# A VectorE duration table, the rank of LayerNorm sums and the place of one product chunk in a Conformer and MLP kernel

## The chip, the core and the metric

One core of a Trainium2 chip runs the whole kernel. It has a matrix engine (TensorE, PE in the rows), a vector engine (VectorE, DVE), an activation engine (ScalarE, ACT), a general engine (GpSimd, POOL) and DMA queues that SyncE (SP) fills. Each engine works through its own list of instructions in order; between engines, semaphores make an instruction wait for what it reads or overwrites. The metric is the device time of one execution in microseconds (us), the median of several runs. Beside the runs stands one profiled execution, and every row below is from that one.

## What is computed

One layer: adaLN modulation, a Conformer convolution module and a squared-ReLU MLP on 1024 tokens of 1024 channels, all in float32. The tokens form segments of 64, and the depthwise convolution stays inside a segment.

```
mod = silu(c) @ w_mod + b_mod          # shift, scale, gate, twice
h = rms_norm(x, norm1_g) * (1 + s1) + sh1
u = h @ w_pw1 + b_pw1                  # pointwise, 1024 -> 2048
a, gate = split(u, 2); u = a * sigmoid(gate)
u = dwconv(u, w_dw) + b_dw             # 31 taps, segments of 64 tokens
u = silu(layer_norm(u, ln_g, ln_b))
x = x + g1 * (u @ w_pw2 + b_pw2)
h = rms_norm(x, norm2_g) * (1 + s2) + sh2
x = x + g2 * (square(relu(h @ w1)) @ w2)   # 1024 -> 4096 -> 1024
out = rms_norm(x, final_g)
```

## The kernel before, in words

**Tiles.** Channels lie on the 128 partitions, tokens along the free side. The tokens form two blocks, A (`b` = 0) and B (`b` = 1), of 512 each; the 1024 channels are eight chunks `c` of 128. A tile `small` is one chunk of one block (128x512), a `bank` one accumulator of PE, a `big` tile a 128x1024 piece of weights or a pair of `small` ones. Each float32 product is three matmuls of parts: hi by hi, hi by lo, lo by hi (L429, L430, L431). "One product" below means these three. The hi part is a cast (weights L391, activations L371 or L568, on ACT), the lo part a subtraction (L378 or L572, on DVE or POOL).

**Stages.** (1) Modulation (L587 on DVE, L595 with L600 on POOL and ACT) and the first RMSNorm. (2) The first pointwise product, a chunk at a time: `first(b, c)` makes 2 x 8 products, which fill two banks, and `gate(b, c)` makes their GLU, a sigmoid on ACT (L631) and a multiplication on DVE (L640). `PW1_ORDER` lists the chunks that run before LayerNorm A; those of `PW1_LATE`, (1, 2) and (1, 3), have a late rank. (3) The depthwise convolution of block A, beside stage 2: of the 31 taps of a chunk, some are diagonal matmuls on PE (`matrix_tap`, L687), some products of ACT (L717) with sums on POOL (L722), the rest multiply-adds of DVE that go in turn to two banks (L732). DVE closes a chunk with two sums (L742, L751). (4) LayerNorm A: `cmean[0]` is a `Mean`. POOL adds the finished chunks 0 to 5 up (L378 on `small` tiles), and PE sums that total, chunk 6 and chunk 7 over the channels, in three feeds of a matrix of ones (L451, two rows of the trace each). DVE subtracts the mean eight times (L766), ACT squares (L493), PE feeds the eight squares (L451 again), ACT takes a root (L505), DVE a reciprocal (L507). 22 small matmuls (L544) stand on PE between. DVE then multiplies (L780), ACT makes the SiLU (L785) and the hi part (L371), DVE the lo part (L378). (5) The second pointwise product of block A: eight output chunks `j` of eight products, each added to x by DVE (L800). (6) The second RMSNorm of A, `norm2`: two feeds on PE (L451), root, reciprocal, L553 and L568 for hi, L572 for lo. (7) The MLP's first product of A (32 chunks, to HBM), with convolution, LayerNorm and second pointwise product of B beside it. (8) The MLP's second product for both blocks, then the final norm.

**The order.** The kernel is not issued in the order in which it is written. Each operation goes into a `plan` with a cost in nanoseconds for its engine (`c_dve`, `c_stt`, `c_act`, `c_pool`) and a rank, `prio`: the number last given to `plan.at`, or one of its own, as the matrix taps have (1030). `plan.run` plays the kernel through with those costs. Whenever an engine is free it takes the operation of the lowest rank among those whose inputs are there in that play. The result is a fixed list for each engine; when the kernel runs, nothing is chosen anew. So a changed cost or rank shows only as another order. Ranks: 1030 matrix taps, 1100 to 1109 the chunks of `PW1_ORDER`, 1200 convolution A, 1300 LayerNorm A, 1400 to 1407 the second pointwise product, 1500 `norm2`, 1600 the late chunks, 2000 on the MLP and block B.

Of the kernel before, what the change touches and what calls it, by code (L numbers as in the profile page):

```python
# [15 lines left out]
KC = D // P  # L16
# [24 lines left out]
PW1_ORDER = (  # L41
    (0, 4), (0, 5), (1, 0), (1, 4), (1, 5),
    (0, 6), (0, 7), (1, 6), (1, 7), (1, 1),
)
PW1_LATE = ((1, 2), (1, 3))
CONV_B = (0, 3, 6, 9, 12, 15, 18, 21)
# [8 lines left out]
CM = (2, 1)  # L55
# [7 lines left out]
S2_ENG, G1_ENG = ("pool", "pool", "dve", "pool", "pool", "pool", "pool", "pool"), ("pool", "pool", "pool", "dve", "dve", "pool", "dve", "pool")  # L63
SH2_ENG, G2_ENG = ("dve", "dve", "dve", "dve", "dve", "dve", "dve", "dve"), "dve"
G1_GATE, S2_GATE = None, None

# [179 lines left out]
def trunk(  # L246
# [50 lines left out]
    def c_dve(n):  # L297
        return 67 + 1.045 * n

    def c_stt(n):  # L300
        return 127 + 1.045 * n

# [137 lines left out]
    class Mean:  # L440

        def __init__(self, b, direct=1, eng="pool", turned=False):
            self.b, self.direct, self.eng, self.turned = b, direct, eng, turned
            self.n, self.sum, self.own, self.acc = 0, None, False, None

        def feed(self, x, first, last):
# [12 lines left out]
            if self.turned:  # L461
                plan.op("pe", 450 * QT, emit_turned, [x, ones], banks(self.acc))
            else:
                plan.op("pe", 1.67 * TB[self.b], emit, [x, ones], banks(self.acc))

# [151 lines left out]
    us, cv, begun = {}, {}, {}  # L617
    cmean = [Mean(0, CM[0]), Mean(1, CM[1])]

# [40 lines left out]
    def conv_start(b, c):  # L660

        u = us[b, c]
        after = [cv[b, c - 2]] if c > 1 else []

        def first_tap(dst, at, k, s):
# [93 lines left out]
    def layer_norm(b, direct):  # L759
        ms = Mean(b, direct, turned=TURNED[1 + 2 * b])  # L760
        for c in range(KC):
# [325 lines left out]

    def first(b, c):
        out = []
        for h in range(2):  # L1090
            acc = acc_of(b, unit=SEG)
            if c < KEPT:
                w_of[c, h] = [wf[k][2 * c + h] for k in range(KC)]
            elif (c, h) not in w_of:
                w_of[c, h] = weights(wpw1[2 * c + h], PW1_LO, (), h1[0][KC - 1 :])
            products(acc, w_of[c, h], h1[b])
            out.append(acc)
        gate(b, c, *out)

    for n, bc in enumerate(PW1_ORDER):  # L1100
        plan.at(1100 + n)
        first(*bc)
    plan.at(1200)
# [142 lines left out]
```

## Time and profile before

| what | value |
|---|---|
| median of 3 runs | 1022.71 us (1021.47 to 1023.96) |
| the profiled execution, its own time | 1022.33 us |
| its span in the trace | 1020.5 us |
| PE busy, share of the span | 980.4 us, 96% |
| DVE busy | 757.2 us, 74% |
| ACT busy | 520.1 us, 51% |
| POOL busy | 513.8 us, 50% |

The profile gives for each engine how long it was busy in a stretch, and the clock granted to PE as a share of full speed. A timeline row has the start, the time, the engine, the source line and operation, what is written and read, and how many instructions were joined. A bracket at its end is idle time just before it, with the instruction that ended it. PE's matmuls overlap: a row of 0.39 us next to one that starts 0.227 us later costs PE 0.227 us. DVE's neighbours overlap a little too, so the cost of a step is the distance between two starts.

### The profile page before, as it was taken

The page shows a single profiled execution, that of the slowest core. Times are in us where ns is not written, and L with a number is a line of the kernel's source. Part 1 is how long each engine was busy: PE and PEld are TensorE (multiplying, and loading weights), DVE is VectorE, ACT ScalarE, POOL GpSimd, SP SyncE. Part 2 cuts the span into 40 slices and gives each one's busy share as a digit, 9 for nine tenths or more (in the row PEclk, how much of TensorE's full clock was granted, in tenths as well). Part 3 has the DMA queues.
Part 4 walks back from the last instruction along what each step waited for, and adds up shares of the span by engine and source line. Part 5 has one row for each costly group of instructions (what it writes and reads, how often), then busy time and mean ns, then how long its engine had stood idle before and what let it go on. Part 6 is the DMA issues. An engine that isn't in the chain of part 4 may idle for free.

```text
span 1020.5 us, 11766 instructions
## 1 busy us (share of the span) xinstructions
PE 980.4 (96%) x4210; PEld 791.7 (78%) x4210; DVE 757.2 (74%) x1008; ACT 520.1 (51%) x748; POOL 513.8 (50%) x328
## 2 busy tenths in 40 slices
PE   5999999959999999999999999999999999999994
PEld 4878787638888888788888888888888888888882
DVE  5999999999699999863464473664747466494887
ACT  6488755185567765582473334342333434252443
POOL 0049999157744544322365536536363653634444
PEclk7999999979999999999999999999999999999998
DMA  9930025444426543644152413123141212303004
GB/s 358 404 114 1 1 83 208 163 164 165 145 83 215 182 158 116 224 157 155 67 192 87 141 41 104 62 83 124 62 144 42 99 66 83 125 1 124 1 1 165
DMA packets 52523, 125.28 MB, mean 123 GB/s; under 512 B 4464, under 2 KB 21104, under 8 KB 52464
## 3 DMA queue, kind: packets, MB, share of 16 engines
q1 hardware_dynamic: 52464, 124.53, 34.7%
q8 instruction: 33, 0.54, 0.2%
q14 instruction: 26, 0.21, 0.1%
HBM read 111.93 MB, written 12.58 MB: 122 GB/s over the span
## 4 chain that ended last, share of the span: by engine, by line
PE 75%; DVE 19%; POOL 2%; issue 2%; ACT 1%; DMA 1%; SPq 0%; POOLq 0%; DVEq 0%; ACTq 0%
PE bank L430 14%; PE bank L431 14%; PE bank L429 14%; DVE bank L732 12%; PE bank L913 10%; PE bank L914 10%; PE bank L912 10%; PE bank L451 2%; DVE big L378 1%; POOL small L378 1%; DVE bank L507 1%; DVE small L751 1%; POOL small L722 1%; DVE big L587 1%; DVE small L640 1%
## 5 line engine op out<-in xcount | busy, mean ns | idle before, releaser
L378 POOL TENSOR_TENSOR big<-big 128x1024 fp32r<-128x1024 f32 (+1 forms) x124 | 299.0, 2421 | 339.0 <-DVE big L378 155.6
L429 PE MATMUL bank<-big 128*128 128x512 f32 x896 | 355.0, 396 | 4.1 <-ACT big L371 3.9
L430 PE MATMUL bank<-big 128*128 128x512 f32 x896 | 350.0, 391 | 4.3 <-DVE big L378 3.2
L431 PE MATMUL bank<-big 128*128 128x512 f32 x896 | 349.7, 390 | 0.0
L800 DVE SCALAR_TENSOR_TENSOR small<-bank,mod,small 128x512 f32<-128x512 f32 x240 | 176.6, 748 | 197.1 <-PE bank L914 158.3
L378 DVE TENSOR_TENSOR big<-big 128x1024 fp32r<-128x1024 f32 (+2 forms) x160 | 198.6, 1262 | 27.4 <-POOL big L378 9.7
L872 ACT CAST big<-big 128x1024 fp32r<-128x1024 f32 x112 | 113.4, 1050 | 193.8 <-POOL big L378 60.0
L430 PEld LDWEIGHTS bank<-big 128*128 128x128 f32 x896 | 168.8, 188 | 42.8 <-DVE big L378 3.7
L732 DVE SCALAR_TENSOR_TENSOR bank<-small,vec,bank 128x464 f32<-128x464 f32 (+11 forms) x318 | 200.5, 697 | 1.7
L429 PEld LDWEIGHTS bank<-big 128*128 128x128 f32 x896 | 168.9, 188 | 41.8 <-ACT big L371 4.1
L431 PEld LDWEIGHTS bank<-big 128*128 128x128 f32 x896 | 168.8, 188 | 35.2
L912 PE MATMUL bank<-big 128*128 128x512 f32 x448 | 174.7, 390 | 0.0
L913 PE MATMUL bank<-big 128*128 128x512 f32 x448 | 174.3, 389 | 0.0
L914 PE MATMUL bank<-big 128*128 128x512 f32 x448 | 174.3, 389 | 0.0
L722 POOL TENSOR_TENSOR small<-small 128x400 f32<-128x400 f32 (+4 forms) x109 | 113.3, 1067 | 50.4 <-DVE big L378 27.8
L391 ACT CAST big<-big 128x1024 fp32r<-128x1024 f32 x92 | 95.6, 1043 | 23.4 <-POOL big L378 11.0
L912 PEld LDWEIGHTS bank<-big 128*128 128x128 f32 x448 | 84.1, 188 | 17.7 <-issue 0.2
L913 PEld LDWEIGHTS bank<-big 128*128 128x128 f32 x448 | 84.1, 188 | 17.6 <-issue 0.2
L914 PEld LDWEIGHTS bank<-big 128*128 128x128 f32 x448 | 84.1, 188 | 17.4
L378 POOL TENSOR_TENSOR small<-small 128x512 f32<-128x512 f32 x39 | 52.1, 1340 | 83.3 <-DVE big L378 44.3
L493 ACT ACTIVATE small<-small 128x512 f32<-128x512 f32 x64 | 39.0, 628 | 64.2 <-DVE small L800 60.0
L717 ACT ACTIVATE small<-small,vec 128x400 f32<-128x400 f32 (+4 forms) x109 | 62.9, 629 | 0.0
(68 smaller groups left out, 597.6 us busy)
## 6 DMA issues: line engine op xcount, KB each, us to landing
big<-in_w SPq DMA_DIRECT2D x96, 512.0 KB, 3.9
big<-in_wmod SPq DMA_DIRECT2D x48, 512.0 KB, 5.4
big<-in_wpw SPq DMA_DIRECT2D x28, 512.0 KB, 5.3
hidden<-small SPq DMA_DIRECT2D x32, 256.0 KB, 2.4
big<-hidden SPq DMA_DIRECT2D x16, 512.0 KB, 3.9
small<-in_xA SPq DMA_DIRECT2D x16, 256.0 KB, 5.2
big<-in_wfirst SPq DMA_DIRECT2D x8, 512.0 KB, 10.2
small<-in_xB SPq DMA_DIRECT2D x16, 256.0 KB, 6.1
```

The costliest lines, as they stand in the source:

```text
L378: lambda: eng_of[o.eng].tensor_tensor(out=out(), in0=a(), in1=b(), op=op), r, w, part=part, port=port,
L391: plan.op("act", c_act(D), lambda: act.copy(t(wh), t(raw)), [raw], [wh], also=[wl])
L429: pe.matmul(o, wh, hi(a)[:, s], start=first, stop=False)
L430: pe.matmul(o, wh, lo(a)[:, s], start=False, stop=False)
L431: pe.matmul(o, wl, hi(a)[:, s], start=False, stop=last)
L722: return pool.tensor_tensor(out=dst, in0=dst, in1=seg(t(m))[:, :, tt], op=ALU.add)
L732: dve.scalar_tensor_tensor(out=dst, in0=src, scalar=w, in1=dst, op0=ALU.mult, op1=ALU.add)
L800: lambda s=s, p=p: dve.scalar_tensor_tensor(out=t(x)[:, s], in0=cut(s, p), scalar=scale.t, in1=t(x)[:, s], op0=ALU.mult, op1=ALU.add,),
L872: plan.op("act", c_act(D), lambda: act.copy(t(h), t(x)), [x], [h], also=[l])
L912: pe.matmul(t(p), t(wh)[:, cs], t(hh)[:, ns], start=first and k == 0, stop=False, skip_group_check=not first)
L913: pe.matmul(t(p), t(wh)[:, cs], t(hl)[:, ns], start=False, stop=False, skip_group_check=not first)
L914: pe.matmul(t(p), t(wl)[:, cs], t(hh)[:, ns], start=False, stop=k == 1, skip_group_check=not first)
```

## The change

Three things change; a fourth, `HOLD_B`, is off and does nothing.

- Chunk (1, 2) leaves `PW1_LATE` and becomes the eleventh of `PW1_ORDER`, with rank 1110; the loads of its weights now wait until chunk (1, 1) has been gated.
- A `Mean` can carry a rank. The three feeds of `cmean[0]` and the eight feeds of LayerNorm A's squares get 1030, above the first product's chunks.
- The plan's cost of a DVE two-operand step rises by 8 ns, that of a DVE multiply-add by 23 ns.

```diff
 PW1_ORDER = (
     (0, 4), (0, 5), (1, 0), (1, 4), (1, 5),
-    (0, 6), (0, 7), (1, 6), (1, 7), (1, 1),
+    (0, 6), (0, 7), (1, 6), (1, 7), (1, 1), (1, 2),
 )
-PW1_LATE = ((1, 2), (1, 3))
+PW1_LATE = ((1, 3),)
+PW1_BACK = 1
...
     def c_dve(n):
-        return 67 + 1.045 * n
+        return 75 + 1.045 * n
...
     def c_stt(n):
-        return 127 + 1.045 * n
+        return 150 + 1.045 * n
...
-        def __init__(self, b, direct=1, eng="pool", turned=False):
+        def __init__(self, b, direct=1, eng="pool", turned=False, prio=None):
+            self.prio = prio
...
-                plan.op("pe", 1.67 * TB[self.b], emit, [x, ones], banks(self.acc))
+                o = plan.op("pe", 1.67 * TB[self.b], emit, [x, ones], banks(self.acc))
+                if self.prio:
+                    o.prio = self.prio
...
-    cmean = [Mean(0, CM[0]), Mean(1, CM[1])]
+    cmean = [Mean(0, CM[0], prio=1030), Mean(1, CM[1])]
...
     def layer_norm(b, direct):
-        ms = Mean(b, direct, turned=TURNED[1 + 2 * b])
+        ms = Mean(b, direct, turned=TURNED[1 + 2 * b], prio=1030 if b == 0 else None)
...
-    def first(b, c):
+    def first(b, c, after=()):
...
-                w_of[c, h] = weights(wpw1[2 * c + h], PW1_LO, (), h1[0][KC - 1 :])
+                w_of[c, h] = weights(wpw1[2 * c + h], PW1_LO, after, h1[0][KC - 1 :])
...
-        first(*bc)
+        first(*bc, [us[PW1_ORDER[n - PW1_BACK]]] if n >= 10 else ())
```

No instruction is added or dropped: only the lists' order changes. In the lists below each row is a source line, an operation, what it writes and reads, its shape, and how many stand in a row.

**DVE, from the end of convolution A to the reciprocal of LayerNorm A, before.** L751 (not shown) has just closed chunk 7; L587 is a modulation step, L732 a tap of block B, L640 the gate of chunk (1, 1), L766 the eight subtractions of the mean, L507 the reciprocal:

```order
L587 ISA big,mod<-big,csil,vec 128x1024
L587 ISA mod 128x1
L1121 TENSOR_SCALAR g1b<-mod,vec 128x1
L732 SCALAR_TENSOR_TENSOR bank<-small,vec,bank 128x8x54
L732 SCALAR_TENSOR_TENSOR bank<-small,vec,bank 128x8x55 x2
L732 SCALAR_TENSOR_TENSOR bank<-small,vec,bank 128x8x56
L640 SCALAR_TENSOR_TENSOR small<-bank,vec,small 128x8x64
L732 SCALAR_TENSOR_TENSOR bank<-small,vec,bank 128x8x56
L732 SCALAR_TENSOR_TENSOR bank<-small,vec,bank 128x8x57
L766 TENSOR_TENSOR small<-small,bank 128x512 x8
```

Ahead of these rows and behind L751 stand three more modulation steps and five column steps (L610, L1121). The same stretch after; the lines are 5 to 7 higher there (L758 closes chunk 7, L773 subtracts, L512 is the reciprocal, L645 the gate, L787 the multiplication):

```order
L758 TENSOR_TENSOR small<-bank,small 128x512
L592 ISA big,mod<-big,csil,vec 128x1024
L592 ISA mod 128x1
L615 TENSOR_SCALAR sc_88<-mod,vec 128x1
L1128 TENSOR_SCALAR g1b<-mod,vec 128x1
L773 TENSOR_TENSOR small<-small,bank 128x512 x8
L739 SCALAR_TENSOR_TENSOR bank<-small,vec,bank 128x8x55 x2
L739 SCALAR_TENSOR_TENSOR bank<-small,vec,bank 128x8x56 x2
L592 ISA big,mod<-big,csil,vec 128x1024
```

Two more modulation steps and a column step follow, then these:

```order
L512 RECIPROCAL bank<-bank 128x512
L645 SCALAR_TENSOR_TENSOR small<-bank,vec,small 128x8x64
L787 TENSOR_TENSOR small<-small,bank 128x512 x8
L1128 TENSOR_SCALAR g1b<-mod,vec 128x1
L615 TENSOR_SCALAR sc_88<-mod,vec 128x1
L739 SCALAR_TENSOR_TENSOR bank<-small,vec,bank 128x8x57
L380 TENSOR_TENSOR big<-small,big 128x512 x3
```

Between the end of the convolution and the subtractions only one modulation step and two column steps are left; one of the six taps and two column steps now stand ahead of L758, the gate of (1, 1) behind the reciprocal. Between subtractions and reciprocal there were two modulation steps, two column steps and five taps; now there are three, one and four.

**PE, at LayerNorm A, before:** all products of `PW1_ORDER`, then the eleven feeds (L451), then the small matmuls:

```order
L431 MATMUL bank<-big 128x512
L451 MATMUL bank<-small,ones 128x512 x11
L544 MATMUL bank<-ones 128x128 x11
L429 MATMUL bank<-big 128x512
```

After, two of the feeds (L454 there) stand far ahead, among the matrix taps (L694) and products of chunks 6 and 7. This is the first of them, for the total of chunks 0 to 5:

```order
L694 MATMUL bank<-small,diag 128x8x51 x2
L694 MATMUL bank<-small,diag 128x8x52
L454 MATMUL bank<-small,ones 128x512
L694 MATMUL bank<-small,diag 128x8x52
L431 MATMUL bank<-big 128x512
```

The feed of chunk 7 stands four products before the end of the first product; three of them follow it, then come the feeds of the squares, the last product and the small matmuls:

```order
L433 MATMUL bank<-big 128x512
L454 MATMUL bank<-small,ones 128x512 x8
L431 MATMUL bank<-big 128x512
L432 MATMUL bank<-big 128x512
L433 MATMUL bank<-big 128x512
L549 MATMUL bank<-ones 128x128 x11
```

The 16 products of chunk (1, 2) stand, after, inside the second pointwise product of A (behind 21 of its 64). Behind the last feed of `norm2` there were 30 products of late chunks; now there are 14.

**DVE, ahead of the reciprocal of `norm2`, after:**

```order
L592 ISA big,mod<-big,csil,vec 128x1024
L592 ISA mod 128x1
L807 SCALAR_TENSOR_TENSOR small<-bank,mod,small 128x512
L380 TENSOR_TENSOR big<-big 128x1024 x2
L512 RECIPROCAL bank<-bank 128x512
L558 SCALAR_TENSOR_TENSOR small<-small,sc_88,bank 128x512 x4
L577 SCALAR_TENSOR_TENSOR big<-small,mod,big 128x512 x4
```

L807 is the last addition to x. Before, a modulation step stood in the place of the two weight splits (L380), and the lo part (L572 there, L577 here) began behind three multiplications instead of four.

## Rows read from the trace of the kernel before

**Rows 1.** Windows: from:to, length, busy us (instructions) by engine, PEclk, DMA share, GB/s.

```profile
65.00:200.00 135.00, 134.47 (x549) 102.31 (x548) 131.91 (x205) 84.83 (x156) 111.97 (x99) 1.00 0.24 85
200.00:234.00 34.00, 20.54 (x60) 11.96 (x59) 33.08 (x56) 25.31 (x40) 16.42 (x11) 0.75 0.42 144
234.00:998.00 764.00, 763.30 (x3348) 627.90 (x3347) 523.71 (x642) 365.64 (x486) 373.09 (x207) 1.00 0.31 108
```

**Rows 2.** Timeline of PE through LayerNorm A.

```profile
199.39 0.39 PE L431 MATMUL bank<-big 128*128 128x512 f32 x1
199.62 2.74 PE L451 MATMUL bank<-small,ones 128*128 128x512 f32 x6
208.66 9.15 PE L451 MATMUL bank<-small,ones 128*128 128x512 f32 x16 [6.30 <-ACT small L493]
...
224.19 0.80 PE L429 MATMUL bank<-big 128*128 128x512 f32 x1 [3.92 <-ACT big L371]
228.23 0.79 PE L430 MATMUL bank<-big 128*128 128x512 f32 x1 [3.24 <-DVE big L378]
```

**Rows 3.** Timeline of DVE, from the end of convolution A.

```profile
197.27 0.20 DVE L610 TENSOR_SCALAR sc<-mod,vec 128x1 f32<-128x1 f32 x1
...
205.27 0.75 DVE L640 SCALAR_TENSOR_TENSOR small<-bank,vec,small 128x512 f32<-128x512 f32 x1
205.93 1.28 DVE L732 SCALAR_TENSOR_TENSOR bank<-small,vec,bank 128x448 f32<-128x448 f32 x2
207.12 4.87 DVE L766 TENSOR_TENSOR small<-small,bank 128x512 f32<-128x512 f32 x8
211.90 1.28 DVE L587 CUSTOM_DVE_ANT_0 big<-big,csil,vec 128x1024 f32<-128x1024 f32 x1
213.10 0.09 DVE L587 DVE_READ_ACCUMULATOR2_ANT mod<- 128x1 f32 x1
...
218.55 3.37 DVE L507 RECIPROCAL bank<-bank 128x512 f32<-128x512 f32 x1 [0.85 <-ACT bank L505]
221.95 4.87 DVE L780 TENSOR_TENSOR small<-small,bank 128x512 f32<-128x512 f32 x8
226.74 0.21 DVE L610 TENSOR_SCALAR sc<-mod,vec 128x1 f32<-128x1 f32 x1
...
227.48 2.50 DVE L378 TENSOR_TENSOR big<-small,big 128x512 fp32r<-128x512 f32 x4
```

**Rows 4.** Chain of waits: start, us, link; taps that follow on one bank.

```profile
132.36 0.70 DVE bank L732
...
133.09 0.71 DVE bank L732
```

**Rows 5.** Timeline of ACT: the last sigmoid before convolution A ends.

```profile
188.94 0.69 ACT L631 ACTIVATE small<-bank,vec 128x512 f32<-128x512 f32 x1 [7.64 <-PE bank L431]
```

**Rows 6.** Timeline of DVE: that sigmoid's gate.

```profile
194.58 0.75 DVE L640 SCALAR_TENSOR_TENSOR small<-bank,vec,small 128x512 f32<-128x512 f32 x1
```

**Rows 7.** Timeline of POOL: the total of chunks 0 to 5, and `norm2`.

```profile
165.35 1.26 POOL L378 TENSOR_TENSOR small<-small 128x512 f32<-128x512 f32 x1
...
272.64 4.72 POOL L378 TENSOR_TENSOR big<-big 128x1024 fp32r<-128x1024 f32 x2
```

**Rows 8.** Timeline of DVE at `norm2`.

```profile
274.95 3.49 DVE L587 CUSTOM_DVE_ANT_0 big<-big,csil,vec 128x1024 f32<-128x1024 f32 x1
...
278.38 3.35 DVE L507 RECIPROCAL bank<-bank 128x512 f32<-128x512 f32 x1
...
283.75 0.75 DVE L572 SCALAR_TENSOR_TENSOR big<-small,mod,big 128x512 fp32r<-128x512 f32 x1
...
293.00 4.63 DVE L378 TENSOR_TENSOR big<-big 128x1024 fp32r<-128x1024 f32 x4
```

**Rows 9.** Timeline of PE at `norm2`: its two feeds.

```profile
274.02 1.02 PE L451 MATMUL bank<-small,ones 128*128 128x512 f32 x2
...
276.25 1.02 PE L451 MATMUL bank<-small,ones 128*128 128x512 f32 x2
```

More of the change, by code (lines that the diff above doesn't have):

```diff
@@ L64 @@
 SH2_ENG, G2_ENG = ("dve", "dve", "dve", "dve", "dve", "dve", "dve", "dve"), "dve"
+HOLD_B = False
 G1_GATE, S2_GATE = None, None
@@ L663, in conv_start @@
         after = [cv[b, c - 2]] if c > 1 else []
+        if b == 1 and c == 0 and HOLD_B:
+            after = [cmean[0].acc[0][1]]
         def first_tap(dst, at, k, s):
```

## Prediction

> **What bounds the kernel now.** I read the windows first. From 65 to 200 us PE is busy 134.47 of 135 us, from 234 to 998 us 763.30 of 764, both at a granted clock of 1.00; from 200 to 234 us it is busy 20.54 of 34 us, at 0.75 [rows 1]. The change neither adds nor drops an instruction, so PE can win only what it loses now, and that lies in one place, LayerNorm A. The timeline of PE says who it waits for there: 6.30 us for ACT's squares, 3.92 us for the first hi part, 3.24 us for the first lo part [rows 2]. These look like three causes. The timeline of DVE shows that they are one queue. Convolution A is done when DVE issues the next thing at 197.27, yet the subtractions of the mean start at 207.12. In the 9.85 us between stand modulation steps, columns, taps of block B and a gate, none of which LayerNorm A needs; the squares could not come sooner. From 207.12 on DVE is busy but for 0.85 us before the reciprocal, until its first lo part at 227.48 lets PE's L430 go at 228.23 [rows 2, 3]. So the time of L430 is the time of DVE's list, and I cost the change by walking through that list in its new order. Everything that PE does after L430 is the same amount of work before and after, so what L430 gains, the end gains, unless a new wait opens behind it.
>
> **The end of convolution A.** The rest of one tap and two columns now stand ahead of it. A tap costs 0.60 (two from 205.93 to 207.12), a column 0.14 (226.74 to 227.48 less a tap): +0.6 + 0.3 = +0.9 [rows 3]. In the new list fewer taps follow a tap on the same bank: 36 instead of 47 in convolution A. Such a follower starts 0.73 us after its predecessor (132.36 to 133.09), where others take 0.60: 11 x 0.13 = -1.4 [rows 3, 4]. Against that, the gates of the first product stand one to eight rows further forward in DVE's list. A gate waits for a sigmoid, hence for PE; the last one before the convolution's end has 189.63 to 194.58, 4.95 us, to spare [rows 5, 6], which is eight taps. Others have less, and each that stands too early stops the taps behind it. The trace does not show these waits. I bound them by nothing and by eight taps, 4.8 us, and take 2.5, between the ends, since most gates move by fewer rows than their slack covers and a wait at one gate makes the next one's shorter. Sum: 197.27 + 0.9 - 1.4 + 2.5 = **199.3**.
>
> **The start of the subtractions.** On DVE one modulation step, 1.20 (211.90 to 213.10), and two columns, 0.3, remain: 199.3 + 1.5 = 200.8. On PE, the feeds were at 199.62 [rows 2]. Now four products (12 matmuls of 0.23, the distance from 199.39 to 199.62: 2.7 us) stand behind the last feed, and two feeds (2.74 / 3 = 0.91 each, 1.8) ahead of it [rows 2]: 199.62 - 2.7 + 1.8 = 198.7. The first early feed needs POOL's total of chunks 0 to 5, which POOL finished at 166.61 [rows 7]; one more weight split, about 2.36 (half of 4.72), now stands ahead of it on POOL [rows 7]. Counting back from 199.62 through the products that stand between, PE reaches that feed near 169 us, which is just when a total that is 2.4 us later ends. I take 1.5 us of waiting, between 0 and 4. What is queued behind the waiting feed is every product behind it, with no idle time to catch up [rows 1]. So the last feed runs from 200.2 to 201.1. DVE and PE come within half a microsecond of each other; I take the later, **201.1**, against 207.12: 6.0 us sooner.
>
> **Subtractions to reciprocal.** Before: 8 subtractions, 4.78 (207.12 to 211.90), two modulation steps, two columns, five taps, then 0.85 us of waiting [rows 3]. Now 4.78, four taps 2.4, three steps 3.6 and a column 0.14: 10.9, so 212.0. The other path, through PE: its first square came 1.54 us after the subtractions began (208.66 less 207.12), eight squares take 16 rows of 0.45 (half of 0.91), 7.3 us at full clock instead of 9.15, and the reciprocal followed 0.74 us behind the last one (217.81 to 218.55) [rows 2, 3]: 201.1 + 1.5 + 7.3 + 0.7 = 210.6. Three products fill PE's wait for the squares. DVE's list is the later of the two: **212.0** against 218.55.
>
> **Reciprocal to L430.** Reciprocal 3.40 (218.55 to 221.95), gate (1, 1) 0.66 (205.27 to 205.93), eight multiplications 4.79 (221.95 to 226.74), two columns 0.3, a tap 0.6, and 0.75 from the start of the first lo part to L430 (227.48 to 228.23) [rows 2, 3]: 212.0 + 10.5 = **222.5**, against 228.23: 5.7 us sooner. By parts: of the 9.85 of filler 8.35 are gone and 0.5 between subtractions and reciprocal; 2.0 come back at the convolution, 0.3 because PE is a little later than DVE, and 0.8 behind the reciprocal, with the gate. The products behind then start at the same low clock as they do now, since PE has an idle stretch before them in either case (0.75 over the window [rows 1]); I cost that at nothing.
>
> **The second pointwise product and chunk (1, 2).** PE has the same products there, with 16 of chunk (1, 2) after the 21st. They need that chunk's split weights, a load and four halves of cast and split, whose load now waits for the gate of (1, 1), at about 216 us by the sum above (212.0 + 3.4 + 0.66). PE gets there near 222.5 + 21 x 0.68 + 4 for the low clock = 241. That leaves 25 us for a load, a cast and a POOL split of 2.36 [rows 7]. I cost it at nothing; the split of the lo parts goes on in DVE's list at 0.60 each [rows 3], and PE asks for one per 0.68 us at the earliest.
>
> **`norm2` without half of its cover.** Call T the end of the last product of the second pointwise product (before: 274.02 [rows 9]). DVE's reciprocal began at T + 4.36, the first lo part at T + 9.7 and ended 0.75 later [rows 8]. PE's last feed stood at T + 2.23 [rows 9], and behind it 30 products, 20.4 us, hid the rest. Now 14 products, 9.5 us, remain: PE wants the first lo part at T + 2.23 + 0.9 + 9.5 = T + 12.6. On DVE two weight splits, 2 x 1.16 (293.00, 4.63 for four) replace the modulation step ahead of the reciprocal, which makes no difference to T + 4.36 (the step took 3.49), and one more multiplication, 0.66, stands ahead of the first lo part [rows 8]: T + 11.2. Margin 1.4 us, stall **0**. Bounds: 0 and 2.5, the price if both splits wait for a cast that follows the root on ACT.
>
> **Sum.** 1022.33 (the profiled execution, 0.38 under the median of the runs) - 5.7 = 1016.6; against the median 1017.0. I take **1016.8**.
>
> **The rivals.**
> (a) *The convolution is late.* If the early gates and the two early feeds cost their upper bounds, the subtractions start 2.5 us later still and the time is about 1019.5; with both ends added up, 1021. For it: DVE is busy 131.91 of 135 us up to there [rows 1] and is the engine that would be stopped. Against: slack such as 4.95 us [rows 5, 6]. The Trainium skill, "TensorE: Matmul & The Clock Gate", Part 2, says that matmuls stay in program order and only weight loads are pulled ahead, and that the other engines' queues are strictly in order; by that rule nothing passes a feed or a gate that waits. No run shows it for these feeds yet.
> (b) *A port.* One modulation step on DVE took 3.49 us (274.95), others 1.28; beside the long one POOL ran two splits of 4.72 that ended at 277.36, and the step ended 1.02 after them [rows 3, 7, 8]. The step thus got going only when POOL was done. Three such steps now stand between subtractions and reciprocal, on the path, where POOL too has splits. Caught once: 2.2 us, 1019.0. Caught three times: 6.6 us, 1023, no gain. Against: 1.28 is the usual figure. The Trainium skill, "GPSIMD Engine Reference", Specifications, states that GpSimd shares its SBUF interfaces with VectorE and that instructions with two SBUF inputs contend; the long step agrees, and by the rule alone every step beside POOL would be hit.
> (c) *Slower: the cover at `norm2` is too short.* The place is PE behind its 14 late products. The margin is 1.4 us; past that every microsecond by which h2's first part is late is lost. From 5.7 + 1.4 = 7.1 us the change makes the kernel slower. It takes two splits that wait for weights or casts, a feed late by POOL, and a step caught at the port (2.2) together in one queue, that of DVE ahead of the reciprocal. Price at 10 us late: 1025.
> (d) *No effect.* LayerNorm A starts as late as before because something that I don't see holds its subtractions: 1022.5.
>
> **How the numbers follow.** Forecast 0.70, spread over 1014 to 1019.5: the lower end is the two waits of 2.5 and 1.5 us at zero, 1014 with PE's part (200.2 instead of 201.1) and a little of a faster restart; (a) 0.13; (b), the full one, 0.06; (c) 0.06; (d) 0.05. A measurement of this kernel tells about 0.2% (2 us) from no change. Faster by that (under 1020.7): forecast and half of (a), 0.77. Slower: (c) and a little of (b), 0.07. Same: 0.16. Range 1014.0 to 1021.2, which leaves out (c), (d), the worst of (b) and a tail below.
>
> **What would show it.** In the changed profile: the subtractions near 201 (right) or past 204 (a); the bracket before the early feed names POOL and is about 1.5 us; the reciprocal near 212, with the modulation steps before it at 1.28 (b: 3.5); L430 near 222.5; no idle PE at the start of the MLP (c: a bracket with DVE's L577). I am wrong if PE has lost time in 65 to 200 us, or in a place after 234 us that was full before.

## Result, and the profile after

The changed kernel takes 1015.17 us (median of 4 runs, 1014.22 to 1015.78), against 1022.49 us: ratio 0.9931, 95% interval 0.9917 to 0.9945, 7.3 us faster. The forecast was 1016.8 us and faster. The profiled execution of after took 1015.36 us with a span of 1013.6, 6.9 us less than before.

The windows of after, with the third stretch of before cut in two (columns as in [rows 1]):

```profile
65.00:200.00 135.00, 133.22 (x542) 101.30 (x541) 130.59 (x206) 84.57 (x153) 111.71 (x99) 1.00 0.22 77
200.00:234.00 34.00, 25.53 (x97) 18.11 (x96) 33.10 (x54) 29.77 (x44) 13.91 (x11) 0.85 0.37 132
234.00:300.00 66.00, 66.00 (x286) 53.26 (x285) 61.59 (x91) 40.37 (x64) 49.56 (x33) 1.00 0.46 168
300.00:998.00 698.00, 697.08 (x3056) 572.98 (x3055) 483.80 (x559) 328.60 (x430) 330.81 (x177) 1.00 0.31 104
```

The same stretch of before, from 234 to 300 us:

```profile
234.00:300.00 66.00, 66.00 (x286) 53.38 (x285) 53.52 (x77) 38.57 (x61) 43.80 (x31) 1.00 0.41 144
```

The count of PE's instructions is the number to look at. By 300 us after has done 542 + 97 + 286 = 925 of them, before 549 + 60 + 286 = 895 (the first two from [rows 1]). Thirty more, at 0.227 us each, are 6.8 us, nearly the whole difference of the spans. After is 7 instructions behind at 200 us, where PE has stopped 1.78 us (first row of the next fence), gains 37 between 200 and 234 us, and from 234 us on PE is as full as before. The next two fences are the timelines of PE and of DVE through LayerNorm A, to be laid beside [rows 2] and [rows 3]:

```profile
198.68 1.10 PE L454 MATMUL bank<-small,ones 128*128 128x512 f32 x2 [1.78 <-DVE small L758]
...
201.70 7.03 PE L454 MATMUL bank<-small,ones 128*128 128x512 f32 x16
...
219.28 0.79 PE L431 MATMUL bank<-big 128*128 128x512 f32 x1 [7.41 <-ACT big L373]
221.13 0.79 PE L432 MATMUL bank<-big 128*128 128x512 f32 x1 [1.06 <-DVE big L380]
```

```profile
197.84 0.69 DVE L758 TENSOR_TENSOR small<-bank,small 128x512 f32<-128x512 f32 x1
198.45 1.28 DVE L592 CUSTOM_DVE_ANT_0 big<-big,csil,vec 128x1024 f32<-128x1024 f32 x1
...
199.90 4.86 DVE L773 TENSOR_TENSOR small<-small,bank 128x512 f32<-128x512 f32 x8
...
210.77 3.36 DVE L512 RECIPROCAL bank<-bank 128x512 f32<-128x512 f32 x1
...
220.25 1.44 DVE L380 TENSOR_TENSOR big<-small,big 128x512 fp32r<-128x512 f32 x2
```

L758 closes the convolution; L773 are the subtractions, at 199.90 instead of 207.12; L512 is the reciprocal, at 210.77 instead of 218.55; L432 (L430 before), the first lo part that PE takes, goes at 221.13 instead of 228.23. A little of that is not the change: after's first modulation step starts at 14.35 us, before's at 14.75, so the trace of after runs 0.4 us ahead from the start (identical lists of two kernels below differ by as much as 0.9 us there).

At `norm2`, timelines of PE, DVE and POOL:

```profile
279.40 1.05 PE L454 MATMUL bank<-small,ones 128*128 128x512 f32 x2
...
281.68 1.02 PE L454 MATMUL bank<-small,ones 128*128 128x512 f32 x2
```

```profile
275.20 2.92 DVE L592 CUSTOM_DVE_ANT_0 big<-big,csil,vec 128x1024 f32<-128x1024 f32 x1
...
284.03 3.37 DVE L512 RECIPROCAL bank<-bank 128x512 f32<-128x512 f32 x1 [0.20 <-ACT bank L510]
...
290.14 2.74 DVE L577 SCALAR_TENSOR_TENSOR big<-small,mod,big 128x512 fp32r<-128x512 f32 x4
```

```profile
274.64 2.41 POOL L380 TENSOR_TENSOR big<-big 128x1024 fp32r<-128x1024 f32 x1 [2.79 <-issue]
277.00 2.28 POOL L380 TENSOR_TENSOR small<-small 128x512 f32<-128x512 f32 x1
```

The feeds have no bracket, and neither has a product behind them. But look at the ends: POOL's total (277.00, 2.28 us) is there at 279.28, and PE takes it at 279.40. There is 0.1 us between a hidden wait and a stop. That row is what the experiments are about.

### The profile page after: what moved, and what is told of

Read it like the earlier page. It is cut to its first block, busy times and chain, and to the rows that moved or that the text cites. A ratio compares the mean times of both kernels' runs of the same rounds, so it can differ in the third digit from the quotient of the medians.

```text
span 1013.6 us, 11767 instructions
## 1 busy us (share of the span) xinstructions
PE 977.7 (96%) x4210; PEld 791.0 (78%) x4210; DVE 771.6 (76%) x1008; ACT 523.2 (52%) x750; POOL 513.6 (51%) x328
## 4 chain that ended last, share of the span: by engine, by line
PE 79%; DVE 15%; issue 2%; ACT 1%; POOL 1%; DMA 1%; SPq 0%; POOLq 0%; DVEq 0%; ACTq 0%
PE bank L432 16%; PE bank L433 16%; PE bank L431 16%; PE bank L921 10%; PE bank L919 10%; PE bank L920 10%; DVE bank L739 9%; DVE big L592 1%; DVE big L380 1%; PE bank L694 1%; PE bank L454 1%; DVE small L758 1%; DVE bank L512 1%; POOL small L380 1%; DMA small<-in_xA 1%
## 5 line engine op out<-in xcount | busy, mean ns | idle before, releaser
L380 POOL TENSOR_TENSOR big<-big 128x1024 fp32r<-128x1024 f32 (+1 forms) x124 | 297.7, 2407 | 332.1 <-DVE big L380 128.9
L431 PE MATMUL bank<-big 128*128 128x512 f32 x896 | 355.9, 397 | 7.5 <-ACT big L373 7.4
L432 PE MATMUL bank<-big 128*128 128x512 f32 x896 | 349.9, 390 | 1.7 <-DVE big L380 1.1
L433 PE MATMUL bank<-big 128*128 128x512 f32 x896 | 349.8, 390 | 0.3 <-DVE big L380 0.3
L807 DVE SCALAR_TENSOR_TENSOR small<-bank,mod,small 128x512 f32<-128x512 f32 x240 | 177.8, 748 | 192.0 <-PE bank L921 156.4
L380 DVE TENSOR_TENSOR big<-big 128x1024 fp32r<-128x1024 f32 (+2 forms) x160 | 213.9, 1358 | 11.8 <-DMA big<-hidden 3.1
L431 PEld LDWEIGHTS bank<-big 128*128 128x128 f32 x896 | 168.8, 188 | 45.6 <-ACT big L373 7.6
L432 PEld LDWEIGHTS bank<-big 128*128 128x128 f32 x896 | 168.8, 188 | 40.2 <-issue 3.2
L433 PEld LDWEIGHTS bank<-big 128*128 128x128 f32 x896 | 168.7, 188 | 36.1 <-DVE big L380 0.8
L729 POOL TENSOR_TENSOR small<-small 128x400 f32<-128x400 f32 (+4 forms) x109 | 113.7, 1066 | 41.4 <-DVE big L380 20.9
L380 POOL TENSOR_TENSOR small<-small 128x512 f32<-128x512 f32 x39 | 52.7, 1356 | 82.1 <-DVE big L380 43.3
```

The source lines that it names most:

```text
L380: lambda: eng_of[o.eng].tensor_tensor(out=out(), in0=a(), in1=b(), op=op), r, w, part=part, port=port,
L431: pe.matmul(o, wh, hi(a)[:, s], start=first, stop=False)
L432: pe.matmul(o, wh, lo(a)[:, s], start=False, stop=False)
L433: pe.matmul(o, wl, hi(a)[:, s], start=False, stop=last)
L729: return pool.tensor_tensor(out=dst, in0=dst, in1=seg(t(m))[:, :, tt], op=ALU.add)
L807: lambda s=s, p=p: dve.scalar_tensor_tensor(out=t(x)[:, s], in0=cut(s, p), scalar=scale.t, in1=t(x)[:, s], op0=ALU.mult, op1=ALU.add,),
```

## Experiments

All kernels below are edits of the changed one (the same 1022.1 to 1022.5 us for before in each group of runs). For each: the median, the ratio to before with its interval, the time at which PE takes its first lo part of LayerNorm A (L432), and PE's instructions done from 65 to 200, to 234 and to 300 us, with their sum.

| kernel | rank | durations | chunk moved | us | ratio, interval | L432 at | done by 300 us |
|---|---|---|---|---|---|---|---|
| before | - | - | - | 1022.3 | | 228.2 | 549 + 60 + 286 = 895 |
| costs_only | - | yes | - | 1018.87 | 0.9966 (0.9952 to 0.9979) | 223.3 | 550 + 78 + 280 = 908 |
| move_only | - | - | yes | 1018.92 | 0.9964 (0.9952 to 0.9977) | 226.0 | 548 + 70 + 286 = 904 |
| rank_only | yes | - | - | 1020.82 | 0.9988 (0.9979 to 0.9997) | 220.7 | 514 + 125 + 262 = 901 |
| old_costs | yes | - | yes | 1017.38 | 0.9954 (0.9942 to 0.9967) | 220.6 | 520 + 120 + 280 = 920 |
| no_rank | - | yes | yes | 1024.80 | 1.0026 (1.0016 to 1.0035) | 226.1 | 551 + 123 + 210 = 884 |
| no_move | yes | yes | - | 1023.11 | 1.0010 (1.0001 to 1.0019) | 221.1 | 542 + 96 + 253 = 891 |
| after | yes | yes | yes | 1015.17 | 0.9931 (0.9917 to 0.9945) | 221.1 | 542 + 97 + 286 = 925 |

The last sum puts the kernels in the order of their times. Of its parts, in the second every kernel beats before; in the third only before, move_only and after are full. So the gain at LayerNorm A is real in all of them, and what differs is how much of it the next stretch takes back.

### One part taken away

**no_rank.**

```diff
-    cmean = [Mean(0, CM[0], prio=1030), Mean(1, CM[1])]
+    cmean = [Mean(0, CM[0]), Mean(1, CM[1])]
...
-        ms = Mean(b, direct, turned=TURNED[1 + 2 * b], prio=1030 if b == 0 else None)
+        ms = Mean(b, direct, turned=TURNED[1 + 2 * b])
```

> The changed kernel without the rank of LayerNorm A's feeds; the moved chunk and the new durations stay. Theory 1 (the length of DVE's list between the convolution's end and the first lo part sets when PE goes on): three modulation steps, two columns and the gate, 4.5 us, stand ahead of the subtractions (they start near 203.0 instead of 199.9), but six multiplications instead of the gate and eight stand behind the reciprocal, so the first lo part lets PE go near 221.2, as in the changed kernel (221.13). In this list 8 products of chunk (1, 2) stand ahead of that point, behind the feeds of the squares; if their weights are there by 213 us they fill idle time, 8 x 0.68 = 5.4 us: 1009.8 us. If those weights come late the gain shrinks, to 1015. Theory 2 (the rank of the feeds is what brings the gain): without it the subtractions come late and the time is 1019 to 1022 us.

Measured: 1024.80 us, slower than before. Up to the first lo part theory 1 is right: it is there at 221.06 (221.2 expected). But all sixteen products of chunk (1, 2) stand ahead of PE's first product of the next stage, not eight; eight of them are behind the small matmuls, so PE takes the lo part at 226.11, without a wait. They did fill idle time: 48 of the 123 instructions from 200 to 234 us are theirs. Then comes this (windows, then the timelines of PE, DVE and POOL):

```profile
234.00:300.00 66.00, 52.68 (x210) 40.85 (x210) 52.83 (x83) 34.93 (x58) 51.72 (x35) 0.90 0.40 144
```

```profile
226.11 0.39 PE L432 MATMUL bank<-big 128*128 128x512 f32 x1
...
253.36 0.80 PE L431 MATMUL bank<-big 128*128 128x512 f32 x1 [9.39 <-DVE small L758]
```

```profile
244.53 7.93 DVE L739 SCALAR_TENSOR_TENSOR bank<-small,vec,bank 128x480 f32<-128x480 f32 x13
252.61 0.69 DVE L758 TENSOR_TENSOR small<-bank,small 128x512 f32<-128x512 f32 x1
253.22 1.52 DVE L380 TENSOR_TENSOR big<-small,big 128x512 fp32r<-128x512 f32 x2
```

```profile
243.40 10.19 POOL L729 TENSOR_TENSOR small<-small 128x408 f32<-128x408 f32 x10
```

PE stops 9.39 us at a hi-by-hi product (L431), the first of the fifth output chunk, which reads no lo part. It writes a bank that block B's convolution holds until L758, a closing sum, has read it. L758 stands behind a row of 13 taps of DVE (22 more stand ahead of that), and it also needs a tap sum from POOL's row of ten, which ends within 0.1 us of DVE's taps. The last two lo parts (L380, 253.22) come only behind L758. Both theories fail on the time: what decides is a place that neither spoke of.

**no_move.**

```diff
-    (0, 6), (0, 7), (1, 6), (1, 7), (1, 1), (1, 2),
+    (0, 6), (0, 7), (1, 6), (1, 7), (1, 1),
...
-PW1_LATE = ((1, 3),)
+PW1_LATE = ((1, 2), (1, 3))
```

> The changed kernel with chunk (1, 2) late again; rank and durations stay. DVE's list through LayerNorm A is the same word for word, PE's up to the second pointwise product too. Theory 1: the move gives nothing by itself here, 1015.2 us, and the first lo part lets PE go at 221.1. Rival (the chunk's products keep PE fed in the second pointwise product, where the first lo parts come slower than PE asks): PE shows idle time between 226 and 250 us that the changed kernel has not, 1017 to 1019 us.

Measured: 1023.11 us. LayerNorm A is the same, L432 at 221.07, and all of its gain is gone. The rival has the stage right, the second pointwise product, but not the stretch (226 to 250 us; the stop ends at 267.15), the wait (a lo part) or the time. Timeline of PE, then of POOL:

```profile
267.15 2.07 PE L454 MATMUL bank<-small,ones 128*128 128x512 f32 x2 [5.37 <-POOL small L380]
```

```profile
264.85 2.25 POOL L380 TENSOR_TENSOR small<-small 128x512 f32<-128x512 f32 x1
```

The first feed of `norm2`, here eight products ahead of the stage's end, waits 5.37 us for POOL's total, and what follows runs at the low clock for a while (granted clock 0.95 from 234 to 300 us, 1.00 in after).

**old_costs.**

```diff
-        return 75 + 1.045 * n
+        return 67 + 1.045 * n
...
-        return 150 + 1.045 * n
+        return 127 + 1.045 * n
```

> The changed kernel with the old durations of DVE; rank and move stay. The feed of chunk 7 stands 13 products before the end of the first product instead of 4, so PE stops for it 6 us sooner. Theory 1: PE's lost time does not count, since the 13 products run in idle time behind the squares' feeds; DVE's list has gate, two columns and one step, 2.1 us, ahead of the subtractions and six multiplications, gate and two multiplications behind the reciprocal: PE goes on near 221, 1015.2 us. Rival (the durations are what brings the gain, since a feed that stands too early for the real DVE stops PE, and the gates that wait for PE then stop DVE): 1018 to 1021 us, with brackets on the feeds of 5 us and more and idle DVE before gates.

Measured: 1017.38 us. Theory 1 was 2.2 us too low, the rival too high. PE did stop more ahead of LayerNorm A (520 instructions instead of 542), the products that it owed ran behind the squares as expected, and L432 came at 220.55. The bracket on chunk 7's feed was 2.11 us, not 5 (timeline of PE):

```profile
196.95 1.10 PE L454 MATMUL bank<-small,ones 128*128 128x512 f32 x2 [2.11 <-DVE small L758]
```

**costs_only.** The table `PW1_ORDER`, `PW1_LATE` and the ranks of before, the new durations.

> The kernel before with the new durations alone. Theory 1: ahead of the subtractions three steps, two columns and the gate, 4.5 us instead of 9.85; between them and the reciprocal four taps, three steps and columns, 6.4 us; eight multiplications, a column and two taps ahead of the first lo part: PE goes on near 224.4 instead of 228.23, 1018.6 us. Theory 2 (the rank brings the gain): 1022 us, no change.

Measured: 1018.87 us, as theory 1 had it (1018.6); L432 at 223.3 (expected 224.4), behind a wait of 3.82 us, where before's was 3.24:

```profile
223.31 0.80 PE L432 MATMUL bank<-big 128*128 128x512 f32 x1 [3.82 <-DVE big L380]
```

The durations alone shorten what stands ahead of the subtractions, because in the play the convolution then ends later and leaves less time to fill. Theory 2 falls.

### Where the gain of no_move went

**no_move_feed.** As no_move; DVE's and POOL's lists are the same up to `norm2`.

```diff
-            self.prio = prio
+            self.prio, self.hold = prio, ()
...
+                o = plan.op("pe", 1.67 * TB[self.b], emit, [x, ones], banks(self.acc), gate=self.hold)
...
         products(acc, w, v)
+        if b == 0 and j == KC - 1:
+            ms.hold = list(acc[0][1].writers)
```

> As no_move, but the first feed of norm2 (the total that POOL adds up) is made to stand behind the last product of the second pointwise product instead of eight products ahead of it; DVE's and POOL's lists are the same up to there. In no_move PE stopped 5.4 us at that feed for POOL, and started again at the low clock. Theory 3 (what LayerNorm A gains is given back at this feed, because POOL's splits, modulation steps and sums of that stretch do not come sooner): the eight products take 5.4 us, the total is there when PE comes, and the time is 1015.5 to 1017 us. Rival (the late chunk itself is what is missing there, for other waits): 1020 us or more, with new brackets between 234 and 300 us.

Measured: 1024.53 us. Theory 3 falls in the form in which I had put it: the place of the feed was not the cause, and its rival (1020 us or more, with new brackets) came true. The wait only went to the next thing that needs POOL. Timelines of PE, ACT, POOL and DVE:

```profile
268.04 0.80 PE L433 MATMUL bank<-big 128*128 128x512 f32 x1 [7.22 <-POOL big L380]
```

```profile
257.28 1.03 ACT L393 CAST big<-big 128x1024 fp32r<-128x1024 f32 x1
```

```profile
255.68 1.06 POOL L729 TENSOR_TENSOR small<-small 128x400 f32<-128x400 f32 x1 [1.66 <-DVE mod L592]
257.98 1.30 POOL L380 TENSOR_TENSOR small<-small 128x512 f32<-128x512 f32 x1 [1.23 <-DVE mod L592]
260.46 0.70 POOL L821 TENSOR_SCALAR small<-small,g1b 128x512 f32<-128x512 f32 x1 [1.19 <-DVE mod L592]
...
265.64 2.34 POOL L380 TENSOR_TENSOR big<-big 128x1024 fp32r<-128x1024 f32 x1
```

```profile
256.09 1.73 DVE L592 CUSTOM_DVE_ANT_0 big<-big,csil,vec 128x1024 f32<-128x1024 f32 x1
...
258.00 2.35 DVE L592 CUSTOM_DVE_ANT_0 big<-big,csil,vec 128x1024 f32<-128x1024 f32 x1
...
261.86 2.69 DVE L592 CUSTOM_DVE_ANT_0 big<-big,csil,vec 128x1024 f32<-128x1024 f32 x1
```

PE's last eight products wait for the lo part of their weights, which ACT had cast at 258.3 and POOL splits at 265.64. Two different things lie between.

POOL has three waits "<-DVE mod L592" of 1.19 to 1.66 us. These are of the kernel's own making: the last lines of `plan.run` let the first POOL step behind a DVE step marked `port` wait for that step, also where it reads nothing of it (the reason given there is "shared port"). The tap sum L729 at 255.68 waits in this way for a modulation step. So a semaphore of this kernel can mean more than that something is read or overwritten.

Beside POOL's steps DVE's modulation steps take 1.73, 2.35 and 2.69 us instead of 1.28, and each ends about 1.1 us behind a POOL step that ran when it began (at 256.74, 259.28 and 263.47). No bracket shows that; it counts as busy time. This is rival (b) of the prediction, met here and not in LayerNorm A. The Trainium skill, "SBUF — State Buffer", SBUF: two separate sides, says that GpSimd and a VectorE instruction with two SBUF inputs hold a shared pair of ports one at a time, for a whole instruction; DVE's rows agree, with up to 1.4 us for one step.

What each of the two costs here is not shown: no run leaves the kernel's own waits out.

**nm_lo7.** As no_move, one split on another engine.

```diff
+LO_ENG = ("pool",) * 7 + ("dve",)
...
-        w = weights(wpw2[j], eng, after)
+        w = weights(wpw2[j], LO_ENG[j] if b == 0 else eng, after)
```

> As no_move, with one operation on another engine: the lo part of the last weights of block A's second pointwise product is split on DVE (1.2 us) instead of POOL (2.4 us). In no_move_feed PE stopped 7.2 us for that split, which POOL reached at 265.6 although the weights had been cast at 258.3; in no_move it stopped 5.4 us at the feed of POOL's total. Theory 4 (POOL's list sets the pace of the second pointwise product once LayerNorm A ends sooner, and the moved chunk only gives PE other work meanwhile): with the split off POOL the stop shrinks to 2 us or less, and the time is 1016 to 1018.5 us without moving the chunk. Rival (PE is short of something else there, the loads or casts of the weights): the stop stays, 1022 us or more.

Measured: 1020.11 us (0.9980, 0.9971 to 0.9989): 3.0 us better than no_move, by one instruction, but not the 5 to 7 expected. The long stop is gone; smaller ones remain (0.74 us at 262.76, 0.43 at 268.47, and these):

```profile
270.59 1.12 PE L455 MATMUL bank<-small,ones 128*128 128x512 f32 x2 [1.00 <-ACT small L499]
...
273.77 0.51 PE L434 MATMUL bank<-big 128*128 128x512 f32 x1 [1.59 <-POOL big L381]
```

So POOL's list does hold PE there. It is not all that does.

**back2** and **b2_s2.** `PW1_BACK = 2`; b2_s2 has five steps of the second scale on DVE besides (the expectation says four fewer on POOL; j = 3 to 7 are five).

```diff
-PW1_BACK = 1
+PW1_BACK = 2
...
-S2_ENG, G1_ENG = ("pool", "pool", "dve", "pool", "pool", "pool", "pool", "pool"), (...)
+S2_ENG, G1_ENG = ("pool", "pool", "dve", "dve", "dve", "dve", "dve", "dve"), (...)
```

> The changed kernel with PW1_BACK = 2: the weights of chunk (1, 2) are loaded after the gate of (1, 7), not of (1, 1), and eight of its products stand inside LayerNorm A, between the squares' feeds and the small matmuls, where the changed kernel's PE was idle for 7.4 us. DVE goes on to the first lo part as before, near 221. By PE's work alone that is 8 x 0.68 = 5.4 us: 1009.8 us. Theory 3: PE now comes to the first feed of norm2 5.4 us sooner, POOL's total (which in the changed kernel ended 0.1 us ahead of PE) does not, so PE waits there about 5 us and the time stays at 1015 us, plus 1 to 2 us for the low clock after the stop.

> As back2 (eight products of chunk (1, 2) inside LayerNorm A), with the modulation steps of the second scale for j = 3 to 7 on DVE (1.2 us each) instead of POOL (2.4 us each and 1.1 us of ACT): four steps fewer on POOL, 9.6 us, five more on DVE, 6 us. In back2 PE stopped 15.7 us at the first feed of norm2 for POOL's total. Theory 4: the stop shrinks by about 10 us, and the time is 1011 to 1014 us, faster than the changed kernel. Rival (DVE has no room for the steps in that stretch, or in block B's LayerNorm behind it): the stop goes but others come, on DVE, and the time is 1018 us or more.

Measured: back2 1022.61 us (1.0002, 0.9993 to 1.0011), b2_s2 1027.68 us (1.0051, 1.0038 to 1.0063). In back2 LayerNorm A costs PE nothing at all between 200 and 234 us, 148 instructions instead of 60, at a clock of 1.00, and the kernel is no faster. Windows, then the timelines of PE and DVE:

```profile
200.00:234.00 34.00, 34.00 (x148) 25.90 (x147) 33.00 (x54) 30.63 (x42) 15.53 (x12) 1.00 0.55 172
```

```profile
277.81 2.08 PE L454 MATMUL bank<-small,ones 128*128 128x512 f32 x2 [15.70 <-POOL small L380]
```

```profile
257.45 6.85 DVE L739 SCALAR_TENSOR_TENSOR bank<-small,vec,bank 128x448 f32<-128x448 f32 x11
...
268.81 1.27 DVE L592 CUSTOM_DVE_ANT_0 big<-big,csil,vec 128x1024 f32<-128x1024 f32 x1
```

The stop at the feed is 15.70 us, three times what theory 3 said. (All sixteen products of chunk (1, 2) stand ahead of the second pointwise product in both kernels, not eight, and twelve products stand between the total's feed and the next one, in after two; so PE comes to the feed sooner than was expected.) DVE has 11 taps of block B at 257.45 and then a row of modulation steps. The third of them (268.81) gives a gate that the seventh chunk of x and so the total need; the others are steps of the second shift, which the total does not need. In b2_s2 the steps of the second scale are on DVE, and the stop is 21.47 us: its rival, that DVE has no room for them and the time is 1018 us or more, came true. POOL is idle there, waiting for steps of the second shift on DVE, again by the kernel's own order:

```profile
283.99 2.07 PE L454 MATMUL bank<-small,ones 128*128 128x512 f32 x2 [21.47 <-POOL small L380]
```

```profile
272.00 1.26 POOL L380 TENSOR_TENSOR small<-small 128x512 f32<-128x512 f32 x1 [2.98 <-DVE mod L592]
277.22 0.69 POOL L821 TENSOR_SCALAR small<-small,g1b 128x512 f32<-128x512 f32 x1 [3.96 <-DVE mod L592]
```

Theory 4, that POOL's load sets the pace, falls in b2_s2, where it was tried: less load on POOL made it worse. What back2 and b2_s2 share is DVE's list: taps of block B, which PE does not yet wait for, stand ahead of the steps that POOL waits for.

**hold0_g.** Gate (1, 1) at rank 1350, lo parts of LayerNorm A at 1290, modulation steps of the second shift and scale from j = 1 behind LayerNorm A.

> The changed kernel with another order inside LayerNorm A: the gate of (1, 1) ranks behind it, lo parts rank ahead of the multiplications, and the modulation steps of the second shift and scale wait for it from j = 1 on. Six multiplications instead of the gate, eight and more stand ahead of the first lo part: PE goes on near 218 instead of 221.1. By PE's work alone 1012 us. Theory 3: POOL's list up to norm2 is longer behind LayerNorm A (the held steps), PE waits for POOL's total at the first feed of norm2, and the gain of 3 us is gone: 1015 us or later.

Measured: 1026.93 us (1.0042, 1.0029 to 1.0054). PE goes on at 218.3, as expected, and the rest goes against both: behind the last feed of `norm2`, in the second half of late chunk (1, 3), it stops 5.88 and 6.63 us for the cast and then POOL's split of that chunk's weights (timeline of PE; lines are one higher here, and L433 at 218.33 is the first lo part):

```profile
289.14 0.80 PE L432 MATMUL bank<-big 128*128 128x512 f32 x1 [5.88 <-ACT big L394]
...
296.99 0.80 PE L434 MATMUL bank<-big 128*128 128x512 f32 x1 [6.63 <-POOL big L381]
```

**move_both.** Chunk (1, 3) in `PW1_ORDER` too.

> The changed kernel with chunk (1, 3) in PW1_ORDER too: no product of a late chunk is left behind the last feed of norm2. The 14 products there took 9.5 us. If they were the cover that the prediction counted (first lo part 8.9 us behind the last feed, margin 1.4 us), PE now stands idle for about 8 us there and starts again at the low clock (2 us): 1023 to 1025 us. Rival (the cover is more than is needed, since POOL's total sets the time anyway, and with 16 more products ahead of it PE no longer waits for POOL): 1015 us.

Measured: 1025.55 us (1.0029, 1.0018 to 1.0039), a little above the expected 1023 to 1025. Behind the last feed, with no product as cover (timeline of PE):

```profile
291.59 1.12 PE L454 MATMUL bank<-small,ones 128*128 128x512 f32 x2 [0.78 <-ACT small L498]
299.10 0.79 PE L431 MATMUL bank<-big 128*128 128x512 f32 x1 [6.38 <-ACT big L573]
```

The wait is 6.38 us for the first hi part and 1.09 for the lo part. The cover that the prediction counted is needed. Rival (c) counted each microsecond of this stop as one of time; here 7.5 us of stop go with 10.4 us more than after.

**rank_only** and **move_only.** One part of the change each, on the kernel before.

> The kernel before with the rank alone: old durations, both late chunks late. LayerNorm A's list on DVE is that of old_costs, which took 1017.4 us with the moved chunk. Theory 4: without the chunk PE runs into POOL's list in the second pointwise product, as no_move did, and the gain is given back: 1021 to 1024 us. Rival (the chunk's place matters only with the new durations): 1017 to 1018 us.

> The kernel before with the moved chunk alone: old durations, no rank. DVE's list is that of the kernel before up to the reciprocal of LayerNorm A (subtractions near 207); behind it the first lo part stands after six multiplications instead of eight, a column and a tap: PE goes on near 226.3 instead of 228.2, 1020.5 us if nothing waits later. Between the changed kernel and no_move the moved chunk was worth 7.9 us. Theory 5 (the chunk is worth something only where PE comes out of LayerNorm A sooner than the other engines' lists can follow, as work that PE does meanwhile; here PE comes out late and has no stop there to fill): 1020 to 1022.5 us. Rival (the chunk is worth 7 to 8 us by itself): 1014 to 1016 us.

Measured: rank_only 1020.82 us, just below the range of theory 4. PE stops for POOL again, at the lo part of the weights:

```profile
264.19 0.50 PE L433 MATMUL bank<-big 128*128 128x512 f32 x1 [2.70 <-POOL big L380]
```

move_only 1018.92 us, between theory 5 (1020 to 1022.5) and its rival: L432 is where it was expected, 226.02, 2.2 us sooner than before; by the counts 9 instructions, 2.0 us, are gained until 300 us, 0.7 of it by the start of the trace (first modulation step at 14.01 instead of 14.75). Of the other 1.4 us, 0.7 is a wait for POOL in block B's LayerNorm that is missing; the rest is open. The chunk is worth 3.4 us there and 7.9 us on top of the other two parts.

## Why the prediction was right

**What bounds the kernel: right.** The three brackets of PE were one queue, DVE's. L432 is 7.1 us sooner (6.7 without the earlier start), the span 6.9, and PE's count says the same.

**The end of the convolution: 199.3 forecast, 198.45 measured** (198.85 with the 0.4 us of the earlier start). The term for the waits at the gates was too high: with the other two terms as forecast, 1.7 to 2.1 us are left for it instead of 2.5. The rows show two new waits of DVE, 1.8 us together, and both brackets name POOL's tap sums, not a sigmoid. The larger is not at a gate but at a closing sum, that of the first chunk (timeline of DVE):

```profile
100.28 0.75 DVE L749 SCALAR_TENSOR_TENSOR small<-bank,vec,small 128x512 f32<-128x512 f32 x1 [1.14 <-POOL small L729]
...
133.99 0.75 DVE L645 SCALAR_TENSOR_TENSOR small<-bank,vec,small 128x512 f32<-128x512 f32 x1 [0.63 <-POOL small L729]
```

So the sum was near, but its reason is at most in part the one given.

**The start of the subtractions: 201.1 forecast, 199.90 measured.** Here the step failed that took PE as the later engine. The early feeds waited at most 0.3 us for POOL, not 1.5; PE was there at 196.90 and stopped 1.78 us for L758, DVE's last sum. DVE set the time: 198.45, a step and two columns, 199.90; PE's feed had ended at 199.78. The prediction's own sign of being wrong, lost time of PE between 65 and 200 us, did come (542 instructions instead of 549). It cost nothing, since the products that PE owed ran in its idle time ahead of the squares and the lo part.

**Subtractions to reciprocal to L432: right to 0.2 us.** Forecast 10.9 and 10.5, measured 10.87 and 10.36. The modulation steps there took 1.20 to 1.21 us from start to start, so rival (b) did not happen in this place.

**The second pointwise product: the step that was missing.** PE came to the moved chunk at 241.1, as forecast (241), but behind 26 of the stage's 64 products, not 21. I costed the chunk at nothing, checked only that its weights come in time, and treated it as lost cover. Without it the kernel takes 1023.1 us and nothing is gained. PE, 7 us sooner, runs into lists of POOL and DVE that are not sooner: modulation, splits of weights, sums of squares. Sixteen products in the middle of the stage, 10.9 us, are the work that PE does meanwhile; POOL's total then ends 0.1 us ahead of its feed. The other kernels agree. Five have the chunk's products inside this stage (after, old_costs, move_only, hold0_g, move_both); once lo parts flow, PE stops at most 0.3 us there, up to the total's feed. In six of the others (no_move, no_move_feed, rank_only, no_rank, back2, b2_s2) it has a stop of 2.7 to 21.5 us there, in nm_lo7 of 0.74 us; in costs_only, whose first lo part comes at 223.3, it has none. That the forecast held all the same was owed to this chunk, not to the argument: it was luck.

**`norm2`: right, by a narrow margin.** First lo part forecast at T + 11.2, measured 290.14 + 0.75 - 279.40 = 11.5. PE took it at T + 12.9 (timeline of PE):

```profile
292.29 0.39 PE L432 MATMUL bank<-big 128*128 128x512 f32 x1
```

No stop, margin 1.4 us, as forecast.

**Open.** Why the play puts taps of block B ahead of the last modulation steps in back2 and b2_s2, and ahead of the last lo parts in no_rank, wasn't tried: loads, slots for raw weights and the modelled port may all bear on it, and no run separates them. No run leaves out the kernel's own waits of POOL for DVE either. nm_lo7 shows that one POOL split is worth 3.0 us in no_move; what holds the remaining 5 us to after was not taken apart. No version that beats after was found.

## What to carry to other kernels

When an engine's idle time is cut at one place, ask at the next places who will be late for it: compute the slack of every input that it takes there, also of those that show no wait today. In a static order an edit's value is not a sum of its parts: here the parts alone gave 3.3, 3.4 and 1.4 us, two of their pairs lost 1.0 and 2.7, the third gave 4.7, and all together 7.3. The count of instructions that the bounding engine has done at a fixed time is a quicker measure of where a gain is kept or lost than its busy share.

## What was not expected of the hardware

In no_move_feed and in after, modulation steps of DVE that start while POOL is in an elementwise step end about 1.1 us behind it; in no_move_feed they took up to 2.69 us instead of 1.28. The profile shows this as busy time, not as a bracket. (The brackets of 1.2 to 1.7 us on POOL there are the kernel's own semaphores.) POOL can lose too: in after, beside one step of 2.92 us (275.20), the last addition of POOL's total took 2.28 us instead of 1.3, which brought it to 0.1 us of its feed.
